# Plain float32 operands in place of products of split float32r parts, in a two-layer diffusion backbone on one core

## The chip, the cores and the metric

One core of a Trainium2 chip runs the whole program, in one launch. The metric is the device time of that launch in microseconds (us), as a median over runs. All inputs and outputs are float32 in the chip's main memory (HBM).

The core's engines are TensorE (PE in the profile, with its weight loads listed apart as PEld), VectorE (DVE), ScalarE (ACT), GpSimd (POOL) and SyncE (SP), which here issues most of the transfers (DMAs). Each engine works through its own list of instructions in order and waits on semaphores for the others.

## What is computed

A backbone of two layers works on 640 tokens of 1024 features: 128 context tokens and 512 latent tokens, which share the weights but have their own modulation (adaLN) and, in the second layer, their own start states.

```
for l in range(2):
    sh1, sc1, g1, sh2, sc2, g2 = split(silu(cond) @ ada_w[l] + ada_b[l], 6)
    h = rmsnorm(x, norm1_g[l]) * (1 + sc1) + sh1
    m = sgu_mixer(h) if l == 0 else rwkv_mixer(h)
    x = x + g1 * m
    h = rmsnorm(x, norm2_g[l]) * (1 + sc2) + sh2
    x = x + g2 * (square(relu(h @ mlp_w1[l])) @ mlp_w2[l])      # 1024 -> 4096 -> 1024
y = rmsnorm(x, final_g)

def sgu_mixer(h):                     # layer 0
    u, v = split(gelu(h @ w_in), 2)   # 1024 -> 2 x 1024
    v = layernorm(v); v = w_s[group] @ v + b_s    # mixes the 128 positions of a chunk
    return (u * v) @ w_out

def rwkv_mixer(h):                    # layer 1: two scans, forward and backward, 16 heads of 64
    xr, xw, xk, xv, xa, xg = [h + shift(h) * mu[j] for j in range(6)]
    r, k, v = xr @ w_r, xk @ w_k, xv @ w_v
    g = sigmoid(xg @ g1) @ g2
    decay, a = low-rank maps of xw and xa, one for each direction   # 1024 -> 64 -> 1024
    y = scan(forward) + scan(backward)   # s = s * w + (s @ -kk) (kk a) + v k;  y = s @ r
    return ((layernorm_of_heads(y) + bonus * v) * g) @ w_o
```

Outputs are the two groups' y and the final scan states of the context.

## The kernel before, in words

Activations lie feature-major: eight tiles of 128 features by 640 tokens. The tokens are taken in two halves, 0 to 256 and 256 to 640 (`HS`). One matmul instruction multiplies a stationary 128x128 weight block with up to 512 moving columns and adds into PSUM.

**The splitting.** float32r is a kind of operand that holds part of a float32 value. Every operand of a large product is cut into a high part (a float32r copy, ScalarE) and a low part (value minus high part, VectorE), and a product of two tiles becomes three matmuls: high by high, high by low, low by high. Weights go through `WPool` (L75): `load` fetches a raw tile of 128x1024, 512 KB, on SP's queue, `split` makes whi and wlo. Activations go through `fill` (L98) or `put` (L1191), which make ahi and alo.

```
85         def split(self, r, n=1024):
88             act.copy(hi[:, :n], r[:, :n])
89             vec.tensor_tensor(out=lo[:, :n], in0=r[:, :n], in1=hi[:, :n], op=ALU.subtract)
...
243            def mm(k, m, hs):
244                (wh, wl), (ah, al) = ws[m], acts[k]
245                for j, (w, x) in enumerate(((wh, ah), (wh, al), (wl, ah))):
246                    mmh(pss[m], w[:, k * P:(k + 1) * P], x, k == 0 and j == 0, k == kt - 1 and j == 2, hs)
```

**Where products of split parts run**, in order of time:

- `sgu` (L287): `zmm` (L302, the matmul is L310) multiplies the 640 tokens with w_in, token-major: five tiles of 128 tokens, stationary, by 512 columns of weights, for 4 blocks of columns and 8 feature tiles. The position mixing (L384) and the transposes after it are plain float32; then `fm` with w_out.
- `fm` (L230) is the general feature-major product, out[n] = W[:, n]^T act: for each output tile n and each of 8 input tiles k, three matmuls on each token half, issued in `mmh` (L112, the matmul is L114). PSUM tiles are called fmps. The weights of the next output tile, or group of tiles, are fetched and split while the present one's products run. `evac` empties PSUM. It serves w_out, both layers' MLPs (`mlp`, L406: 32 output tiles for w1, then w2 in four blocks) and the RWKV layer's k projection.
- `rwkv_project` (L462): the first products of the low-rank maps (L507, PSUM tile l1ps) are plain float32 on 255 and 385 columns. `hidden` (L519) splits their result by putting high and low parts in the two halves of the partitions. `mixed` (L536) makes the shifted inputs and splits them. Then a loop over the eight feature tiles t takes r (`rmm`, L733), v (`vmm`, L744, one step behind, 256 columns) and the second low-rank products (`lora2`, L608: L624 with high weights on all 128 rows, L625 with low weights on 64 rows), whose steps are woven between the others; `finish` (L691) and `prep` (L630) prepare the scans on VectorE, ScalarE and GpSimd. Meanwhile GpSimd works at the first scan group's triangular inverse (`inv_sub`, L838).
- `rwkv_core` (L810): the scans, eight groups (four pairs of feature tiles by two directions), all in plain float32 (L910, L1026 to L1054, and the inverses' L962 and L980). Class `Tail` (L1205) weaves the gates (g2) and the product with w_o into the last two groups by a table of positions, in `early`, `gate`, `late`, `last` and `end`; its products of three go through `mm3` (L1178, the matmul is L1180), its splits through `put` and `Tail.split` (L1221). `ahead` (L1294) fetches and splits the first two w1 tiles of the second MLP, from four halves.

The adaLN products (L122, L323, L1166) are plain float32 with a stationary operand of 32 columns. Buffers come from pools with a fixed count for each kind: 5 raw and 4 split weight pairs in the first part, 3 and 2 in the projections, 4 and 3 in the second MLP. The order of instructions on an engine follows the program with priorities for a few urgent stretches.

Of the kernel before, what the change touches and what calls it, by code (L numbers as in the profile page):

```python
# [7 lines left out]
F32 = mybir.dt.float32  # L8
F32R = mybir.dt.float32r
AF = mybir.ActivationFunctionType  # L10
ALU = mybir.AluOpType
# [4 lines left out]
P = 128  # L16
# [12 lines left out]
def tile_trunk(ctx: ExitStack, tc: tile.TileContext, a: dict):  # L29
# [45 lines left out]
    class WPool:  # L75
        def __init__(self, stack, tag, nraw, nsp, **kw):
            self.raw = Pool(stack, f"wr{tag}", {"r": nraw}, **kw)
            self.sp = Pool(stack, f"ws{tag}", {"h": nsp, "l": nsp}, **kw)

        def load(self, src, n=1024):  # L80
            r = self.raw.tile([P, 1024], F32, tag="r", name="wraw")
            nc.sync.dma_start(out=r[:, :n], in_=src)
            return r

        def split(self, r, n=1024):
            hi = self.sp.tile([P, 1024], F32R, tag="h", name="whi")
            lo = self.sp.tile([P, 1024], F32R, tag="l", name="wlo")
            act.copy(hi[:, :n], r[:, :n])  # L88
            vec.tensor_tensor(out=lo[:, :n], in0=r[:, :n], in1=hi[:, :n], op=ALU.subtract)  # L89
            return hi, lo  # L90

        def get(self, src, n=1024):
            return self.split(self.load(src, n), n)

    def parts(pool, tags=("ah", "al")):
        return pool.tile([P, T], F32R, tag=tags[0], name="ahi"), pool.tile([P, T], F32R, tag=tags[1], name="alo")

    def fill(pt, src, r=(0, T)):  # L98
        hi, lo = (x[:, r[0]:r[1]] for x in pt)
        act.copy(hi, src)  # L100
        vec.tensor_tensor(out=lo, in0=src, in1=hi, op=ALU.subtract)  # L101

    def split_act(pool, src, tags=("ah", "al")):
        pt = parts(pool, tags)
        fill(pt, src)
        return pt
# [10 lines left out]
    def ada_steps(wp, l, u, ui):  # L117
# [8 lines left out]
        tm = wp.sp.tile([P, 16, 32], F32, "h", "adat")  # L126
# [31 lines left out]
    class Norm:  # L158
# [19 lines left out]
        # in two steps, with room for other products while the first one's result is worked on  # L178
# [27 lines left out]
        def apply(self, k, bc, l, w, h, dst=None):  # L206
            r = HS[h]
            if dst is None:
                dst = self.pool.tile([P, 384], F32, tag="nh", name="nh")[:, :r[1] - r[0]]
# [1519 lines left out]
```

## Time and profile before

| what | value |
|---|---|
| runs | 2085.41, 2088.6, 2097.09 us; median 2088.6 |
| profiled execution | span 2109.0 us, from first to last instruction; the page gives no other time for it |
| mean granted TensorE clock | 0.937 |
| TensorE busy | 1991.5 us of 15882 matmul records |
| VectorE, ScalarE, GpSimd busy | 1162.9, 774.5, 389.3 us |
| HBM | 214.67 MB read, 45.22 MB written |

By stage, from the profile's windows (us from the span's start):

| stage | from - to | TensorE busy | VectorE busy | granted clock |
|---|---|---|---|---|
| first norm, gating layer's w_in | 0 - 160 | 143.4 | 73.7 | 1.00 |
| position mixing | 160 - 187 | 25.5 | 17.6 | 1.00 |
| w_out, first MLP | 187 - 705 | 516.6 | 202.0 | 1.00 |
| entry of the RWKV layer | 705 - 764 | 40.9 | 53.0 | 0.80 |
| k projection | 764 - 823 | 58.7 | 45.3 | 0.97 |
| projection loop | 823 - 1072 | 214.8 | 173.5 | 0.84 |
| scans, with the tail's products from 1468 on | 1072 - 1640 | 538.3 | 416.4 | 0.87 |
| second MLP | 1640 - 2086 | 445.0 | 168.5 | 1.00 |
| final norm and output | 2086 - 2109 | 8.4 | 13.0 | 0.71 |

How to read it: times are those of one profiled execution. A matmul's record has a start and a modelled end, and records overlap, so a busy TensorE need not be at its peak; the distance from start to start of neighbouring records says more than their length. The clock is the share of full speed that the throttle granted TensorE. The chain of work is followed back from the last instruction, at each step to what released it; what lies beside the chain costs nothing. "L114" is line 114 of the kernel, and where a helper issues all matmuls, tiles' names tell its callers apart.

### The profile page before, as it was taken

The page shows a single profiled execution, that of the slowest core. Times are in us where ns is not written, and L with a number is a line of the kernel's source. Part 1 is how long each engine was busy: PE and PEld are TensorE (multiplying, and loading weights), DVE is VectorE, ACT ScalarE, POOL GpSimd, SP SyncE. Part 2 cuts the span into 40 slices and gives each one's busy share as a digit, 9 for nine tenths or more (in the row PEclk, how much of TensorE's full clock was granted, in tenths as well). Part 3 has the DMA queues.
Part 4 walks back from the last instruction along what each step waited for, and adds up shares of the span by engine and source line. Part 5 has one row for each costly group of instructions (what it writes and reads, how often), then busy time and mean ns, then how long its engine had stood idle before and what let it go on. Part 6 is the DMA issues. An engine that isn't in the chain of part 4 may idle for free.

```text
span 2109.0 us, 39157 instructions
## 1 busy us (share of the span) xinstructions
PE 1991.5 (94%) x15882; PEld 1739.6 (82%) x15882; DVE 1162.9 (55%) x2308; ACT 774.5 (37%) x1737; POOL 389.3 (18%) x689
## 2 busy tenths in 40 slices
PE   6999999999999789988869999999998999999997
PEld 5777889999999678877747766767787999999996
DVE  5435643333333796766786577787658533333334
ACT  5323531312222255444524444554434522222231
POOL 0000000000000200477551465465201000000000
PEclk9999999999999889987869879998799999999998
DMA  8777352222222033554655444552242222222221
GB/s 286 265 266 233 105 184 80 71 81 70 80 71 75 36 96 121 171 151 129 186 159 175 143 131 148 166 160 80 71 130 76 67 74 75 76 74 77 73 67 51
DMA packets 124438, 254.58 MB, mean 121 GB/s; under 512 B 24417, under 2 KB 63969, under 8 KB 124129
## 3 DMA queue, kind: packets, MB, share of 16 engines
q1 hardware_dynamic: 123824, 251.62, 37.3%
q8 instruction: 125, 2.05, 0.4%
q14 instruction: 57, 0.46, 0.1%
q10 hardware_dynamic: 432, 0.46, 0.1%
HBM read 214.67 MB, written 45.22 MB: 123 GB/s over the span
## 4 chain that ended last, share of the span: by engine, by line
PE 85%; DVE 6%; POOL 3%; ACT 2%; issue 2%; DMA 1%; SPq 0%; DVEq 0%; POOLq 0%; ACTq 0%
PE fmps L114 47%; PE zps L310 6%; PE p L910 4%; PE wops L1180 3%; PE vps L751 2%; PE za L1039 2%; PE za L1026 2%; PE sy L1053 2%; PE sy L1034 1%; PE rps L114 1%; PE trps L932 1%; PE adaps L1166 1%; PE adaps L122 1%; PE sy L1036 1%; PE tps L980 1%
## 5 line engine op out<-in xcount | busy, mean ns | idle before, releaser
L114 PE MATMUL fmps<-ahi,whi 128*128 128x256 f32 (+1 forms) x2272 | 534.6, 310 | 4.9 <-ACT ahi L100 3.1
L114 PE MATMUL fmps<-alo,whi 128*128 128x256 f32 (+1 forms) x2272 | 533.8, 309 | 1.3 <-DVE alo L101 1.3
L114 PE MATMUL fmps<-ahi,wlo 128*128 128x256 f32 (+1 forms) x2272 | 533.8, 309 | 0.0
L114 PEld LDWEIGHTS fmps<-ahi,whi 128*128 128x128 f32 x2272 | 414.4, 188 | 11.0 <-ACT ahi L100 6.3
L114 PEld LDWEIGHTS fmps<-alo,whi 128*128 128x128 f32 x2272 | 415.0, 188 | 2.1 <-DVE alo L101 1.8
L114 PEld LDWEIGHTS fmps<-ahi,wlo 128*128 128x128 f32 x2272 | 415.2, 188 | 1.0 <-issue 0.8
L88 ACT CAST whi<-wraw 128x1024 fp32r<-128x1024 f32 x174 | 182.6, 1050 | 632.6 <-PE fmps L114 538.2
L89 DVE TENSOR_TENSOR wlo<-wraw,whi 128x1024 fp32r<-128x1024 f32 x174 | 214.4, 1233 | 276.2 <-ACT whi L88 276.1
L283 DVE SCALAR_TENSOR_TENSOR x<-fmps,mod,x 128x128 f32<-128x128 f32 (+2 forms) x153 | 74.5, 527 | 305.4 <-PE fmps L114 305.4
L491 POOL TENSOR_TENSOR xx<-h 128x254 f32<-128x254 f32 (+1 forms) x16 | 12.1, 754 | 721.2 <-DVE h L210 706.1
L841 POOL TENSOR_TENSOR inv<-inv 128x220 f32<-128x220 f32 (+29 forms) x217 | 100.7, 464 | 114.4 <-DVE inv L834 57.7
L910 PE MATMUL p<-W,IT 128*128 128x256 f32 x320 | 109.6, 453 | 10.0 <-DVE B L925 5.9
L843 POOL TENSOR_TENSOR inv<-inv 128x220 f32<-128x220 f32 (+29 forms) x217 | 104.5, 482 | 16.9
L1042 ACT ACTIVATE RZ<-za 64x64 f32<-64x64 f32 x320 | 58.4, 214 | 66.7 <-PE za L1039 53.9
L1060 DVE TENSOR_TENSOR RZ<-sy,PC 64x64 f32<-64x64 f32 x256 | 49.4, 219 | 60.2 <-PE sy L1054 52.5
L101 DVE TENSOR_TENSOR alo<-rsq,ahi 128x640 fp32r<-128x640 f32 (+2 forms) x69 | 53.6, 776 | 45.6 <-ACT ahi L100 45.3
L100 ACT CAST ahi<-rsq 128x640 fp32r<-128x640 f32 (+2 forms) x69 | 47.5, 689 | 82.2 <-DVE rsq L435 81.8
L910 PEld LDWEIGHTS p<-W,IT 128*128 128x128 f32 x320 | 57.9, 211 | 22.9 <-DVE B L925 6.3
L1054 PE MATMUL sy<-RZ,B 128*64 128x64 f32 x640 | 72.6, 251 | 0.6 <-ACT RZ L1042 0.6
L1026 PEld LDWEIGHTS za<-RZ,W 128*64 128x64 f32 x640 | 43.5, 154 | 33.8 <-DVE RZ L1060 9.0
L1026 PE MATMUL za<-RZ,W 128*64 128x64 f32 x640 | 62.5, 254 | 8.4 <-DVE RZ L1080 5.9
L1036 PE MATMUL sy<-RZ,W 128*64 128x64 f32 x640 | 69.1, 249 | 0.0
(289 smaller groups left out, 3428.4 us busy)
## 6 DMA issues: line engine op xcount, KB each, us to landing
wraw<-w SPq DMA_DIRECT2D x126, 512.0 KB, 3.5
wraw<-ada SPq DMA_DIRECT2D x64, 512.0 KB, 4.9
W<-dKR SPq DMA_DIRECT2D x80, 256.0 KB, 3.5
adaw<-adac SPq DMA_DIRECT2D x32, 512.0 KB, 4.4
dKR<-zero SPq DMA_DIRECT2D x32, 320.0 KB, 6.3
dKR<-KR SPq DMA_DIRECT2D x32, 320.0 KB, 4.1
dIT<-IT SPq DMA_DIRECT2D x16, 640.0 KB, 3.3
IT<-dIT SPq DMA_DIRECT2D x80, 128.0 KB, 2.9
```

Of the source, the lines that this page charges most:

```text
L88: act.copy(hi[:, :n], r[:, :n])
L89: vec.tensor_tensor(out=lo[:, :n], in0=r[:, :n], in1=hi[:, :n], op=ALU.subtract)
L114: pe.matmul(ps[:, PS0 + t0:PS0 + t1], w, x[:, t0:t1], start=start, stop=stop)
L283: vec.scalar_tensor_tensor(out=X[n][:, t0:t1], in0=ps[:, t0 - r[0]:t1 - r[0]], scalar=mod[l][:, which, n, g:g + 1], in1=X[n][:, t0:t1], op ...
L310: pe.matmul(pss[i], x[:, i * P:(i + 1) * P], w[:, kq * 512:(kq + 1) * 512], start=(k == 0 and j == 0), stop=(k == KT - 1 and j == 2))
L841: eng.tensor_tensor(out=tv, in0=LA[:, s + 1:32, s:s + 1].to_broadcast([P, n, m]), in1=LX[:, s:s + 1, c0:c1].to_broadcast([P, n, m]), op=AL ...
L843: eng.tensor_tensor(out=LX[:, s + 1:32, c0:c1], in0=LX[:, s + 1:32, c0:c1], in1=tv, op=ALU.subtract)
L910: pe.matmul(ps[:, :, 2 * e:2 * e + 2].rearrange("p h s t -> p h (s t)"), IT[:, e], W[:, :, 2 * e:2 * e + 2].rearrange("p h s t -> p h (s t ...
L1026: pe.matmul(za[a0:a0 + 64, 0], W[:, h, 3 * e], RZ[:, ti, h, c], start=True, stop=True)
L1036: pe.matmul(sy[y0:y0 + 64, h], W[:, h, 1 + e], RZ[:, ti, h, c], start=h == 0, stop=False)
L1054: pe.matmul(sy[y0:y0 + 64, h], B[:, h, 3 * e], RZ[:, ti, h, c], start=False, stop=h == 1)
L1180: pe.matmul(ps, u, v, start=start and j == 0, stop=stop and j == 2)
```

## The change

All operands of products are plain float32; nothing is split. Weight tiles are used where they land, and one matmul stands where three stood. `split`, `get`, `parts`, `fill`, `split_act`, `mm3`, `put`, `Tail.split` and their tiles are gone; `acts` makes activation tiles, `Tail.load` loads. What had been written to a tile and then split is written straight to the operand: the norm's `apply`, the MLP's square (the tile rsq is gone), the mixed inputs, the gated y, the hidden values of the low-rank maps. Scores, scans, adaLN products and norms' statistics stay. The core of the diff:

```diff
     class WPool:
-        def __init__(self, stack, tag, nraw, nsp, **kw):
-            self.raw = Pool(stack, f"wr{tag}", {"r": nraw}, **kw)
-            self.sp = Pool(stack, f"ws{tag}", {"h": nsp, "l": nsp}, **kw)
+        def __init__(self, stack, tag, n, **kw):
+            self.raw = Pool(stack, f"w{tag}", {"r": n}, **kw)
...
-        def split(self, r, n=1024):
-            hi = self.sp.tile([P, 1024], F32R, tag="h", name="whi")
-            lo = self.sp.tile([P, 1024], F32R, tag="l", name="wlo")
-            act.copy(hi[:, :n], r[:, :n])
-            vec.tensor_tensor(out=lo[:, :n], in0=r[:, :n], in1=hi[:, :n], op=ALU.subtract)
-            return hi, lo
...
+    def acts(pool, n=1):
+        return [pool.tile([P, T], F32, tag="a", name="a") for _ in range(n)]
...
             def mm(k, m, hs):
-                (wh, wl), (ah, al) = ws[m], acts[k]
-                for j, (w, x) in enumerate(((wh, ah), (wh, al), (wl, ah))):
-                    mmh(pss[m], w[:, k * P:(k + 1) * P], x, k == 0 and j == 0, k == kt - 1 and j == 2, hs)
+                mmh(pss[m], ws[m][:, k * P:(k + 1) * P], xs[k], k == 0, k == kt - 1, hs)
...
                     for i in range(5):
-                        for j, (w, x) in enumerate(((wh, ah), (wh, al), (wl, ah))):
-                            pe.matmul(pss[i], x[:, i * P:(i + 1) * P], w[:, kq * 512:(kq + 1) * 512],
-                                      start=(k == 0 and j == 0), stop=(k == KT - 1 and j == 2))
+                        pe.matmul(pss[i], hs[k][:, i * P:(i + 1) * P], wcur[0][:, kq * 512:(kq + 1) * 512],
+                                  start=k == 0, stop=k == KT - 1)
...
-    MB = (4, 3, 11)
+    MB = (12, 11)
...
                     r = mp.tile([P, T], F32, tag="r", name="relu")[:, :m]
                     act.activation(out=r, in_=ps, func=AF.Relu)
-                    q = mp.tile([P, T], F32, tag="q", name="rsq")[:, :m]
-                    vec.tensor_tensor(out=q, in0=r, in1=r, op=ALU.mult)
                     if n not in ss:
-                        ss[n] = parts(sp)
-                    fill(ss[n], q, rg)
+                        ss[n], = acts(sp)
+                    vec.tensor_tensor(out=ss[n][:, rg[0]:rg[1]], in0=r, in1=r, op=ALU.mult)
...
-            wp = WPool(el, "p", 3, 2)
+            wp = WPool(el, "p", 7)
...
-                            pe.matmul(ps, hi[:, 2 * x + d], hw[:, sl], start=True, stop=False)
-                            pe.matmul(ps, lo[a0:a0 + 64, 2 * x + d], hw[a0:a0 + 64, sl], start=False, stop=True)
+                            pe.matmul(ps, w[a0:a0 + 64, 2 * x + d], hid[x][a0:a0 + 64, sl], start=True, stop=True)
...
-            def rmm(t, raw, z):
-                wh, wl = wp.split(raw)
+            def rmm(t, w, z):
                 ps = pp.tile([P, 1024], F32, "f", "rps")
                 for k in range(KT):
-                    ah, al = xrs[k]
-                    for j, (w, x) in enumerate(((wh, ah), (wh, al), (wl, ah))):
-                        mmh(ps, w[:, k * P:(k + 1) * P], x, k == 0 and j == 0, k == KT - 1 and j == 2)
+                    mmh(ps, w[:, k * P:(k + 1) * P], xrs[k], k == 0, k == KT - 1)
...
-                    self.rings = {"x": (F32, 4, []), "r": (F32, 4, []), "o": (F32, 3, []), "s": (F32R, 6, [])}
+                    self.rings = {"x": (4, []), "r": (4, []), "o": (3, []), "s": (3, [])}
...
+                def load(self, src, n, keep=None):
+                    r = buf(keep, [P, 512], F32, "wos") if keep else self.tmp(n, "s")
+                    nc.sync.dma_start(out=r[:, 0:n], in_=src)
+                    return [r[:, c:c + P] for c in range(0, n, P)]
...
                             for k in range(4):
-                                mm3(ps, ws[n][k], self.ys[k][h], k == 0, k == 3)
+                                pe.matmul(ps, ws[n][k], self.ys[k][h], start=k == 0, stop=k == 3)
...
                 def ahead(self):
-                    w = xw.tile([P, 4, 1024], F32R, "w", "w1s")
-                    nn.pre = [(w[:, 0], w[:, 1]), (w[:, 2], w[:, 3])]
...
+                    w = xw.tile([P, 4, 1024], F32, "w", "w1s")
+                    nn.pre = [w[:, n] for n in range(3)]
+                    for n in range(3):
+                        nc.sync.dma_start(out=nn.pre[n], in_=a["w1"][1, n])
+                        yield
...
-        wp = WPool(es, "a", 5, 4)
+        wp = WPool(es, "a", 12)
```

`vmm` changes like `zmm`, `end` and `finish` of `Tail` like its other products; `WPool(es, "b", MB[0])` of the second MLP holds 12 tiles.

More of the change, by code (lines that the diff above doesn't have):

```diff
@@ L75, in tile_trunk, with tile @@
     class WPool:
-        def __init__(self, stack, tag, nraw, nsp, **kw):
-            self.raw = Pool(stack, f"wr{tag}", {"r": nraw}, **kw)
-            self.sp = Pool(stack, f"ws{tag}", {"h": nsp, "l": nsp}, **kw)
+        def __init__(self, stack, tag, n, **kw):
+            self.raw = Pool(stack, f"w{tag}", {"r": n}, **kw)
+        def tile(self):
+            return self.raw.tile([P, 1024], F32, tag="r", name="w")
         def load(self, src, n=1024):
-            r = self.raw.tile([P, 1024], F32, tag="r", name="wraw")
+            r = self.tile()
             nc.sync.dma_start(out=r[:, :n], in_=src)
             return r
-        def split(self, r, n=1024):
-            hi = self.sp.tile([P, 1024], F32R, tag="h", name="whi")
-            lo = self.sp.tile([P, 1024], F32R, tag="l", name="wlo")
-            act.copy(hi[:, :n], r[:, :n])
-            vec.tensor_tensor(out=lo[:, :n], in0=r[:, :n], in1=hi[:, :n], op=ALU.subtract)
-            return hi, lo
[L92 to L106, printed above, removed]
+    def acts(pool, n=1):
+        return [pool.tile([P, T], F32, tag="a", name="a") for _ in range(n)]
     def segs(r):
@@ L600, in ahead @@
             def ahead(t):
[L601 removed]
+                l2 = ev_.tile([P, 512], F32, "lr", "l2")
                 nc.sync.dma_start(out=l2, in_=a["l2"][t])
@@ L608, in lora2 @@
             def lora2(raw, tiles):
[L609 to L613 removed]
+                w = raw.rearrange("p (a b) -> p a b", a=4)
                 yield
@@ L1174, in ada_core @@
                 gamma(1, 1)
-            def mm3(ps, w, x, start, stop):
-                for j, (u, v) in enumerate(((w[0], x[0]), (w[0], x[1]), (w[1], x[0]))):
-                    pe.matmul(ps, u, v, start=start and j == 0, stop=stop and j == 2)
             def bank(n, tag="p"):
@@ L1212, in tmp @@
                 def tmp(self, n, ring="r"):
-                    dt, size, tiles = self.rings[ring]
+                    size, tiles = self.rings[ring]
                     if len(tiles) < size:
-                        t = buf("B", [P, 512], dt, "tmp")
+                        t = buf("B", [P, 512], F32, "tmp")
                     else:
```

170 lines of the change are left out of this document (55 added, 115 removed).

## The prediction

> **What bounds the kernel now.** The page comes first: who is busy, and what the chain of work that ended last consists of.
>
> ```profile
> span 2109.0 us, 39157 instructions
> PE 1991.5 (94%) x15882; PEld 1739.6 (82%) x15882; DVE 1162.9 (55%) x2308; ACT 774.5 (37%) x1737; POOL 389.3 (18%) x689
> PEclk9999999999999889987869879998799999999998
> ...
> PE 85%; DVE 6%; POOL 3%; ACT 2%; issue 2%; DMA 1%; SPq 0%; DVEq 0%; POOLq 0%; ACTq 0%
> PE fmps L114 47%; PE zps L310 6%; PE p L910 4%; PE wops L1180 3%; PE vps L751 2%; PE za L1039 2%; PE za L1026 2%; PE sy L1053 2%; PE sy L1034 1%; PE rps L114 1%; PE trps L932 1%; PE adaps L1166 1%; PE adaps L122 1%; PE sy L1036 1%; PE tps L980 1%
> ...
> wraw<-w SPq DMA_DIRECT2D x126, 512.0 KB, 3.5
> ```
>
> The reader is to see that TensorE holds 85% of the chain, and that one helper line, L114 (the products of `fm`), holds 47% of the span. Busy time alone proves little for a pipelined engine, so the second view is the list of waits (engine and line, for whom; total, times, longest): do the splits pace the products, or the products the splits?
>
> ```profile
> ACT whi L88 <- PE fmps L114: 538.2, 123, 13.2
> DVE wlo L89 <- ACT whi L88: 276.1, 79, 7.1
> ...
> PE fmps L114 <- ACT ahi L100: 3.1, 1, 3.1
> ...
> PE fmps L114 <- DVE alo L101: 2.1, 3, 1.0
> ```
>
> ScalarE waits 538 us for TensorE to give split buffers back; TensorE waits some 5 us for splits in `fm`. The splits are hidden there, and the products are the pace. So the question is what one product costs in each form.
>
> **Price of the old form.** The chain in order of time (start, length, what) has long unbroken runs of it:
>
> ```profile
> 53.16 17.69 PE zps L310 x75
> ...
> 1649.05 436.45 PE fmps L114 x2974
> ```
>
> 436.45 / 2974 = 0.1468 us a record, mean over 256 and 384 columns (0.459 ns a column). Call a 128x128 weight block with all 640 tokens a pair of `fm`: three products, two token halves, six records, 0.881 us. For `zps` (512 columns) a product is 17.69 / 75 = 0.236 us, a pair of tiles 0.708.
>
> **Price of the new form.** Some products are plain float32 already, the low-rank ones of L507 for one. Rows: groups by shape over the whole span and over 748.5 to 757.5, the stretch's engine times, and two rows of the timeline (start, length from first start to last end, count).
>
> ```profile
> L507 PE MATMUL l1ps<-xq,wraw 128*128 128x385 f32 x48 | 19.3, 566 | 9.9 <-DVE xq L477 9.9
> ...
> 748.50:757.50 9.00, 9.00 (x29) 5.28 (x28) 8.74 (x14) 5.35 (x7) 0.00 (x0) 1.00 0.40 104
> ...
> L507 PE MATMUL l1ps<-xq,wraw 128*128 128x385 f32 x29 | 9.5, 487 | 0.0
> ...
> L507 PEld LDWEIGHTS l1ps<-xq,wraw 128*128 128x128 f32 x28 | 5.3, 190 | 3.7
> ...
> 748.30 3.07 PE L507 MATMUL l1ps<-xq,wraw 128*128 128x385 f32 x9
> ...
> 1122.19 1.13 PE L910 MATMUL p<-W,IT 128*128 128x256 f32 x4
> ```
>
> The code has 3 x 8 = 24 such products of 385 columns and the trace 48 records: a plain product leaves two, each with a weight load. Nine in a row take 3.07 us; without the last one's 0.487 that is 2.58 / 8 = 0.323 us from start to start, 0.839 ns a column. Granted clock 1.00. The four records of L910 bear it out: three gaps of 256 x 0.839 = 0.215 leave 1.13 - 0.64 = 0.49 for the last. The weight loads take no time of their own: 28 of them are busy 5.28 of 9 us beside a TensorE busy 9.00. A 256-column record, 0.215 us, still covers a load of 0.190; without that cover each of a pair's four records would add up to 0.19.
>
> So a pair of `fm` becomes 2 x 640 x 0.839 ns = 1.074 us instead of 0.881: +0.193. Two records at nearly twice the column price replace three: 22% more, not a third less.
>
> **The change part by part.** Counts of products (one form of three is shown, so its count is that of pairs; the 256-column half stands for both):
>
> ```profile
> L114 PE MATMUL fmps<-alo,whi 128*128 128x256 f32 x1136 | 318.1, 280 | 1.3 <-DVE alo L101 1.3
> L114 PE MATMUL fmps<-alo,w1s 128*128 128x256 f32 x16 | 4.5, 283 | 0.0
> ...
> L310 PE MATMUL zps<-whi,alo 128*128 128x512 f32 x160 | 63.9, 399 | 0.0
> L751 PE MATMUL vps<-whi,alo 128*128 128x256 f32 x160 | 50.1, 314 | 0.0
> L625 PE MATMUL zps<-hw,l2l 64*128 64x320 f32 x64 | 28.0, 449 | 3.0 <-DVE l2l L612 3.0
> L114 PE MATMUL rps<-alo,whi 128*128 128x256 f32 x64 | 20.5, 320 | 0.0
> ```
>
> 1. `fm` (w_out, both MLPs, wk): 1136 + 16 = 1152 pairs. At 0.881 they make 1014 us, and the chain gives L114 47% of 2109 = 991: all on the path. 1152 x 0.193 = **+222**.
>
> One page of the Trainium skill speaks against this price. By the Trainium skill, "FP8 and Floating Point Precision", section TensorE Precision Notes, true float32 takes four passes through the array, where the reduced kind reads the 4-byte value and truncates it; with one pass for the reduced kind the ratio is 4 to 3, an estimated 1.174 us a pair, and this term +338. The measured column prices (0.839 x 2 against 0.459) give 3.66 to 3, and the sum goes by them; the other is a rival below.
>
> 2. `zmm` in the gating layer: 160 pairs, 2 x 512 x 0.839 = 0.859 against 0.708: 160 x 0.151 = **+24**. All on the path: 160 x 0.708 = 113 us is 5.4% of the span, and the chain gives L310 6%.
>
> 3. The projection loop (r, v, second low-rank products; 823 to 1072 us). Views: the stretch, the chain's shares in it, and the first and last of the nine splits that lie on its chain.
>
> ```profile
> 823.00:1072.00 249.00, 214.78 (x1279) 178.84 (x1278) 173.47 (x150) 124.61 (x199) 142.83 (x180) 0.84 0.52 154
> ...
> by line: PE vps L751 20.3%; PE rps L114 11.9%; issue 10.8%; PE zps L625 7.0%; POOL AT L841 5.0%; PE zps L624 3.9%; POOL inv L843 3.6%; DVE IT L665 3.5%; DVE IT L663 3.3%; DMA S<-kk 2.8%; PE rbps L114 2.5%; PE bops L726 2.4%; POOL PC L645 2.
> ...
> 836.67 0.94 ACT whi L88
> ...
> 1059.95 1.13 DVE wlo L89
> ...
> 861.11 0.28 PE L751 MATMUL vps<-whi,alo 128*128 128x256 f32 x1
> ...
> 865.91 0.28 PE L751 MATMUL vps<-wlo,ahi 128*128 128x256 f32 x1
> ```
>
> No single engine paces this: chains through VectorE, GpSimd and TensorE alternate, at a granted clock of 0.84. Streaming at full clock: r 64 x 0.193 = 12.4; v, from 0.120 a product (40 starts in 4.80 us), 160 x (0.429 - 0.360) = 11.1; low rank 64 x (2 x 320 x 0.839 ns - 2 x 0.147) = 15.6, since two split records become two plain ones of nearly double length. Together 39, at clock 0.84 46. The chain holds 43.1% of 249 = 107 us of these products, whose streaming is (56.4 + 57.6 + 18.8) / 0.84 = 158: 68% of them. So 0.68 x 46 = 31. From the chain go nine splits, 9.4 us together. Net **+22**; ends -9 (products hidden, splits gone) and +46. VectorE also loses splits off the chain there, which I count at nothing: what is late next is `prep`'s long products (L663, L665).
>
> 4. The tail, 1490 to 1650 (gates and w_o during and after the last scans). By the code 8 + 64 = 72 pairs.
>
> ```profile
> by line: PE wops L1180 44.4%; PE za L1026 6.6%; PE fmps L114 6.0%; PE za L1039 5.4%; PE sy L1053 4.7%; PE sy L1034 4.3%; PE sy L1036 2.6%; PE sy L1054 2.3%; issue 2.1%; PE ytps L1131 1.8%; DVE nh L210 1.7%; DMA tmp<-wo 1.6%; PE tps L980 1.6
> ...
> 1582.44 0.76 DVE alo L1193
> ...
> 1609.31 0.43 DVE yp L1193
> ```
>
> 44.4% of 160 us is 71, at least the 72 x 0.881 = 63 of streaming: on the path. +13.9, less nine splits on the chain from the first to the last row shown, 5.3 us: **+9** (ends -5 and +14). Here loads of w_o reach TensorE without a stop at ScalarE, VectorE or GpSimd, but a load now waits until products release its tile; ring `s` holds three tiles where it held three pairs of parts.
>
> 5. Splits that stand on the chain elsewhere, 14 rows:
>
> ```profile
> 24.09 0.71 ACT ahi L100 x2
> ...
> 1648.66 0.34 DVE alo L101
> ```
>
> 2.4 us before the first `zps`, 3.5 between the mixing products (ScalarE's copy from PSUM stays), 3.5 at the entry of the RWKV layer, 2.7 at the second MLP's first tiles: **-12**. What is late next there is the normalization's own activation.
>
> 6. All other splits, buffers and transfers: 0. The four large groups of splits:
>
> ```profile
> L88 ACT CAST whi<-wraw 128x1024 fp32r<-128x1024 f32 x174 | 182.6, 1050 | 632.6 <-PE fmps L114 538.2
> L89 DVE TENSOR_TENSOR wlo<-wraw,whi 128x1024 fp32r<-128x1024 f32 x174 | 214.4, 1233 | 276.2 <-ACT whi L88 276.1
> L101 DVE TENSOR_TENSOR alo<-rsq,ahi 128x640 fp32r<-128x640 f32 (+2 forms) x69 | 53.6, 776 | 45.6 <-ACT ahi L100 45.3
> L100 ACT CAST ahi<-rsq 128x640 fp32r<-128x640 f32 (+2 forms) x69 | 47.5, 689 | 82.2 <-DVE rsq L435 81.8
> ```
>
> ScalarE loses 230 us and VectorE 268 in them, and `fm`'s part of it lies under its products, as the waits showed: those 5 us are all that could come back. Weights are loaded a tile ahead; a tile now lasts 8 x 1.074 = 8.6 us, and a load lands in 3.5 (the page's last line above). Were that cover gone, each tile would add the difference to TensorE's queue, where every later product stands behind it. On SP's queue nothing is moved past a scan's load but `ahead`'s: three whole w1 tiles in the last scan instead of four half ones, and one load fewer in the MLP behind it. The scans keep their products and are costed at nothing.
>
> Sum: 222 + 24 + 22 + 9 - 12 = +265. On the profiled execution: 2109 + 265 = 2374. The page gives its span alone, 20.4 us above the median of the runs, 2088.6; I carry the difference over: 2088.6 + 265 = **2354 us**, slower by 13%.
>
> **The rivals.**
> Four records' worth at the old price: if plain products in dense streams cost 4/3 of three split ones, term 1 grows by 116, `zps` by 13, the loop by 14, the tail by 7: 2354 + 150 = 2504. For it: 0.839 was seen in stretches of microseconds, not hundreds. Against: the old form shows one column price in both (0.469 in 5 us of `vps`, 0.459 in 436 us of `fm`), and the clock row is 1.00 in the plain stretch. (It is what the section of the Trainium skill named in step 1 would give.)
>
> Loop and tail hide their longer products: the loop gives -9 and the tail -5, 265 - 31 - 14 = 220: 2309. For it: VectorE's 70% and the mixed chain of the loop. Against: 43% of that chain is these very products.
>
> The other side, faster: the L507 rows are paced by their feed, not by TensorE, and a plain record streams at the old column price. For it: VectorE is busy 8.74 of those 9 us, making each moving tile. Then a pair costs four records, 4 x 0.147 = 0.587: 1152 x -0.294 = -338, `zps` -38, splits -27: near 1686. It decides from a record below 0.688 ns a column (0.881 / 1280) on. Against: a product's two records share their operands, so the second needs no feed, yet L910 shows the same spacing inside four records whose tiles were all there. That the products don't change form at all is excluded by the diff.
>
> **How the numbers follow.** Forecast 0.78; hidden loop and tail 0.13; 4/3 price 0.05; faster 0.02; the rest, mostly a tail or loop slower than costed, 0.02. The loop's and tail's ends (-31 / +24, -14 / +5), another 10 us for the column price and the runs' own spread give 2300 to 2405, which leaves out the 4/3 case and the faster one. About 0.5%, 10 us, is what this measurement tells from no change: faster 0.02, within 0.01, slower 0.97.
>
> **What would show it.** Right: L114's `fmps` in one form, 4608 records, 0.215 and 0.322 us apart, two MLP stretches of some 550 us each instead of 451; whi, wlo, ahi, alo gone; ScalarE less busy by 230 us or more and VectorE by 268 or more; the chain still TensorE's. Wrong: records below 0.18 or above 0.23 us apart at 256 columns, TensorE idle between `fm`'s tiles behind a weight DMA, or a granted clock below 0.95 inside the MLPs.

## The result, and the profile after

The changed kernel takes 2308.66 us (median of runs from 2306.0 to 2312.76) against 2092.85 for the kernel before (2085.41 to 2108.12, the runs on the same chip): a ratio of 1.1006 with a 95% interval of 1.0951 to 1.106, slower by 216 us between the medians. The forecast was 2354 in a range of 2300 to 2405. The sign and the size of the large terms came out; the projection loop and the tail came out with the wrong sign.

The page of the changed kernel: span, busy time of the engines, granted clock in 40 slices, shares of the chain, the group of `fm`, and the weight loads (last number: us from issue to landing).

```profile
span 2304.2 us, 32383 instructions
PE 2237.5 (97%) x12982; PEld 1506.4 (65%) x12982; DVE 823.3 (36%) x1942; ACT 492.4 (21%) x1367; POOL 368.7 (16%) x677
PEclk9999999999999988998989998999999999999998
PE 94%; DVE 2%; DMA 1%; ACT 1%; POOL 1%; issue 1%; SPq 0%; DVEq 0%; POOLq 0%; ACTq 0%
...
L95 PE MATMUL fmps<-a,w 128*128 128x384 f32 (+1 forms) x4512 | 1218.2, 433 | 1.5 <-ACT lh L496 1.3
...
w<-w SPq DMA_DIRECT2D x125, 512.0 KB, 3.4
```

VectorE lost 339.6 us of work and ScalarE 282.1; TensorE has 2900 records fewer and is busy 246 us longer. It now holds 94% of the chain (85% before). With 96 further records on the tiles w1s, `fm` has the 4608 that were forecast, and the group shown waits 1.5 us in all. The chain in order of time has the price:

```profile
51.31 21.66 PE zps L283 x50
...
830.60 5.09 DMA w<-g
...
1749.91 529.13 PE fmps L95 x1968
```

529.13 / 1968 = 0.2689 us a record where the old form had 0.1468. A pair of `fm` (four records) takes 1.0755 us; 1.074 was forecast. For `zps`, 21.66 / 50 = 0.433 a record, 0.430 forecast.

By stage, in the two traces, from TensorE's first record of one stage to its first record of the next (us; the last two columns are differences). The entry and the final norm are counted from the last record ahead of them, and the loop ends with its last `vps` record:

```
stage                                     before   after   measured   forecast
start to first zps                          27.9    23.6     -4.3       -2.4
w_in (zps)                                 133.6   157.8    +24.2      +24
position mixing                             23.3    20.6     -2.7       -3.5
w_out, first MLP                           523.5   631.7   +108.2     +111
entry of the RWKV layer                     54.9    57.1     +2.2       -3.5
k projection                                61.6    71.7    +10.1      +12
projection loop                            244.4   229.3    -15.1      +22
last vps to first scan step                 13.1    15.5     +2.4        0
first scan group                            91.8    71.5    -20.3        0
scan groups 2 to 6                         295.4   299.6     +4.2        0
last two groups, and tail behind them      161.7   149.4    -12.3       +9
second MLP                                 460.8   559.2    +98.4      +96
final norm                                  16.7    17.3     +0.6        0
```

The dense stages agree with their forecast within some 3 us each. Most of the deviation stands in three rows: loop, first scan group, tail. Here they are in the windows of the kernel before and then of the changed one. Columns: stretch, its length, busy time (records) of TensorE, weight loads, VectorE, ScalarE, GpSimd, then the granted clock, DMA share and GB/s.

```profile
824.90:1069.40 244.50, 211.87 (x1259) 177.41 (x1260) 170.85 (x146) 122.09 (x195) 141.72 (x178) 0.84 0.52 155
1069.40:1082.50 13.10, 3.16 (x14) 2.05 (x12) 12.35 (x19) 1.21 (x4) 1.17 (x3) 0.72 0.77 213
1082.50:1174.40 91.90, 84.89 (x912) 61.85 (x912) 60.05 (x173) 35.40 (x136) 28.83 (x64) 0.82 0.49 150
...
1469.80:1591.70 121.90, 117.84 (x1352) 95.10 (x1353) 80.22 (x246) 51.37 (x190) 27.61 (x44) 0.87 0.33 100
1591.70:1631.50 39.80, 35.81 (x235) 32.28 (x231) 31.81 (x98) 16.82 (x44) 4.23 (x3) 0.96 0.17 54
```

```profile
962.50:1191.80 229.30, 228.28 (x969) 149.38 (x966) 136.13 (x121) 103.64 (x171) 126.67 (x171) 0.94 0.54 156
1191.80:1207.30 15.50, 8.90 (x35) 5.90 (x33) 14.58 (x19) 2.72 (x6) 12.19 (x15) 0.67 0.78 252
1207.30:1278.70 71.40, 69.95 (x895) 53.12 (x894) 53.68 (x174) 34.06 (x136) 30.24 (x59) 1.00 0.63 186
...
1578.30:1690.00 111.70, 111.40 (x1276) 75.72 (x1274) 66.63 (x227) 35.78 (x161) 19.53 (x44) 0.96 0.37 116
1690.00:1727.70 37.70, 37.70 (x171) 26.88 (x166) 25.85 (x84) 12.07 (x32) 0.00 (x0) 1.00 0.05 15
```

In the loop TensorE was busy 211.87 of 244.5 us at a clock of 0.84, and is now busy 228.28 of 229.3 at 0.94. Busy time times clock is 178 us before and 215 after: the 37 us of additional streaming (39 forecast) are there. They filled the 32.6 us in which TensorE had waited, and the clock rose. The question for the experiments was what shortens the loop, and what the first scan group, whose own products did not change, has to do with it.

### The profile page after: what moved, and what is told of

It is laid out like the page before. It is cut to its first block, busy times and chain, and to the rows that moved or that the text cites. A ratio compares the mean times of both kernels' runs of the same rounds, so it can differ in the third digit from the quotient of the medians.

```text
span 2304.2 us, 32383 instructions
## 1 busy us (share of the span) xinstructions
PE 2237.5 (97%) x12982; PEld 1506.4 (65%) x12982; DVE 823.3 (36%) x1942; ACT 492.4 (21%) x1367; POOL 368.7 (16%) x677
## 4 chain that ended last, share of the span: by engine, by line
PE 94%; DVE 2%; DMA 1%; ACT 1%; POOL 1%; issue 1%; SPq 0%; DVEq 0%; POOLq 0%; ACTq 0%
PE fmps L95 54%; PE zps L283 6%; PE p L856 4%; PE vps L698 3%; PE rps L95 3%; PE zps L578 2%; PE za L972 2%; PE za L985 2%; PE wops L1188 2%; PE sy L999 2%; PE wops L1284 2%; PE sy L980 1%; PE trps L878 1%; PE adaps L1112 1%; PE l1ps L477 1%; PE tps L926 1%
## 5 line engine op out<-in xcount | busy, mean ns | idle before, releaser
L95 PE MATMUL fmps<-a,w 128*128 128x384 f32 (+1 forms) x4512 | 1218.2, 433 | 1.5 <-ACT lh L496 1.3
L95 PEld LDWEIGHTS fmps<-a,w 128*128 128x128 f32 x4512 | 856.2, 190 | 361.2 <-ACT lh L496 1.8
L405 ACT ACTIVATE relu<-fmps 128x640 f32<-128x640 f32 (+2 forms) x70 | 45.8, 657 | 903.2 <-PE fmps L95 903.0
L408 DVE TENSOR_TENSOR a<-relu 128x640 f32<-128x640 f32 (+2 forms) x70 | 53.6, 768 | 490.3 <-ACT relu L405 490.0
L283 PE MATMUL zps<-w,a 128*128 128x512 f32 x320 | 141.9, 598 | 0.0
L787 POOL TENSOR_TENSOR inv<-inv 128x220 f32<-128x220 f32 (+29 forms) x217 | 105.7, 487 | 72.1 <-DVE inv L780 36.5
L283 PEld LDWEIGHTS zps<-w,a 128*128 128x128 f32 x320 | 59.4, 190 | 78.2 <-issue 74.0
L789 POOL TENSOR_TENSOR inv<-inv 128x220 f32<-128x220 f32 (+29 forms) x217 | 105.6, 487 | 16.9
L95 PE MATMUL rps<-a,w 128*128 128x256 f32 (+1 forms) x256 | 82.9, 478 | 0.0
L698 PE MATMUL vps<-w,h 128*128 128x256 f32 x320 | 77.4, 389 | 0.0
L698 PEld LDWEIGHTS vps<-w,h 128*128 128x128 f32 x320 | 58.3, 190 | 20.1 <-issue 12.9
L95 PEld LDWEIGHTS rps<-a,w 128*128 128x128 f32 x256 | 51.7, 209 | 30.1 <-issue 12.6
L972 PEld LDWEIGHTS za<-RZ,W 128*64 128x64 f32 x640 | 42.3, 144 | 32.6 <-issue 9.1
```

The lines of the kernel that those rows point to most:

```text
L95: pe.matmul(ps[:, PS0 + t0:PS0 + t1], w, x[:, t0:t1], start=start, stop=stop)
L283: pe.matmul(pss[i], hs[k][:, i * P:(i + 1) * P], wcur[0][:, kq * 512:(kq + 1) * 512], start=k == 0, stop=k == KT - 1)
L408: vec.tensor_tensor(out=ss[n][:, rg[0]:rg[1]], in0=r, in1=r, op=ALU.mult)
L698: pe.matmul(pss[i // 2][:, i % 2], xvs[k][:, i * P:(i + 1) * P], w[:, kq * 256:(kq + 1) * 256], start=(k == 0 and i % 2 == 0), stop=(k == ...
L787: eng.tensor_tensor(out=tv, in0=LA[:, s + 1:32, s:s + 1].to_broadcast([P, n, m]), in1=LX[:, s:s + 1, c0:c1].to_broadcast([P, n, m]), op=AL ...
L789: eng.tensor_tensor(out=LX[:, s + 1:32, c0:c1], in0=LX[:, s + 1:32, c0:c1], in1=tv, op=ALU.subtract)
```

## The experiments

### One part at a time

Four kernels exchange the projection loop, or loop and tail, between the two forms. `mid_split` and `loop_split` have the dense stages plain, as in the changed kernel, `mid_plain` and `loop_plain` have them split, as in the one before. The exchange, shown for the r projection (v, the low-rank products and, in the tail, `mm3` alike):

```diff
-            def rmm(t, raw, z):
-                wh, wl = wp.split(raw)
+            def rmm(t, w, z):
...
-                    ah, al = xrs[k]
-                    for j, (w, x) in enumerate(((wh, ah), (wh, al), (wl, ah))):
-                        mmh(ps, w[:, k * P:(k + 1) * P], x, k == 0 and j == 0, k == KT - 1 and j == 2)
+                    mmh(ps, w[:, k * P:(k + 1) * P], xrs[k], k == 0, k == KT - 1)
```

`mid_split`, the dense stages plain, loop and tail split:

> The changed kernel with the projection loop and the tail put back to products of split parts; the dense products stay plain. Stages of the two known traces: the changed kernel is 15 us shorter in the loop, 16 in the scans and 14 in the tail than before, where the forecast had +22, 0 and +9. Theory A (these 45 us come from the loop's and the tail's own change): the loop is about 244 us again, the tail 122, and the time 2309 + 45 = 2354. Theory B (they come from what lies around: clock left over from the longer dense streams, earlier weights, a lighter VectorE elsewhere): loop near 229 and time within 10 of 2309.

`loop_split`, all plain but the loop:

> The changed kernel with only the projection loop (r, v, second low-rank products) put back to split parts. Theory A: loop 244 us instead of 229, and the first scan group 92 instead of 71, if that group's gain is a late effect of the loop: 2309 + 15 + 16 = 2340; if the scans' gain is not the loop's, 2309 + 15 = 2324. Theory B: within 8 of 2309.

`mid_plain`, the dense stages split, loop and tail plain:

> The kernel before with the loop's and the tail's products plain; the dense products (gating layer, w_out, MLPs, k projection) stay split. Theory A: 2093 - 45 = 2048, loop about 229, tail about 112, granted clock in the loop 0.94 instead of 0.84. Theory B: within 10 of 2093; and by the forecast's own terms (+22, +9) 2124.

`loop_plain`, all split but the loop:

> The kernel before with only the loop's products plain. Theory A: 2093 - 15 - 16 = 2062 if the first scan group's gain follows the loop, 2078 if not. By the forecast's term 2115. Theory B: within 8 of 2093.

Measured, beside 2090.86 for the kernel before on that chip:

```
kernel       loop    tail    median us   ratio to before (95%)     loop   first scan group   last two groups
mid_split    split   split   2329.3      1.1122 (1.1062-1.1181)    239.6       91.7              111.9
loop_split   split   plain   2323.69     1.1094 (1.1038-1.115)     239.5       91.8              111.3
mid_plain    plain   plain   2070.05     0.9887 (0.983-0.9945)     231.0       71.6              111.6
loop_plain   plain   split   2081.56     0.9939 (0.9912-0.9965)    231.0       71.6              113.1
```

Making only the dense stages plain costs 2329.3 - 2090.86 = 238 us, where the terms of `fm`, `zmm` and the splits elsewhere make 234. A plain loop gains 9 us with the dense stages split (2090.86 - 2081.56) and 15 with them plain (2323.69 - 2308.66); loop and tail together gain 21 in both cases. The 2308.66 is from the round above, where the kernel before took 2 us longer, so differences with it are uncertain by about that much. Neither "they cost 31" nor "they cost nothing" is what happens. Theory A had the stages right and the times too far apart (45 and 31 us, where 21 and 9 to 15 came): its differences were those of the two traces, and that of the kernel before is longer than any of its timed runs. `loop_split` came out at the 2324 that was expected if the scans' gain were not the loop's, yet its first scan group took 91.8 us, so that agreement is luck. The first scan group follows the form of the loop ahead of it: 92 us behind a split loop, 71 to 72 behind a plain one. And `mid_plain` is faster than both kernels.

### What sets the loop

`dead_splits` puts back the work of the splits for ScalarE and VectorE without the use of their results: in the changed kernel's loop, w_r, w_v and the second low-rank weights are cut into two parts that no product reads. `few_tiles` takes the buffers back to three weight tiles and one low-rank tile. `lr_twice` issues each of the 64 second low-rank products twice into the same PSUM tile.

```diff
+            def cast(r, n):
+                hi = dead.tile([P, 1024], F32R, "h", "dhi")[:, 0:n]
+                lo = dead.tile([P, 1024], F32R, "l", "dlo")[:, 0:n]
+                act.copy(hi, r[:, 0:n])
+                vec.tensor_tensor(out=lo, in0=r[:, 0:n], in1=hi, op=ALU.subtract)
```

```diff
-            wp = WPool(el, "p", 7)
+            wp = WPool(el, "p", 3)
...
-            ev_ = Pool(el, "rpv2", {"vs": 2, "lr": 2})
+            ev_ = Pool(el, "rpv2", {"vs": 2, "lr": 1})
```

```diff
-                            pe.matmul(ps, w[a0:a0 + 64, 2 * x + d], hid[x][a0:a0 + 64, sl], start=True, stop=True)
+                            for _ in range(2):
+                                pe.matmul(ps, w[a0:a0 + 64, 2 * x + d], hid[x][a0:a0 + 64, sl], start=True, stop=True)
```

> The changed kernel, with the loop's splits of weights (w_r, w_v, second low-rank weights) made again by ScalarE and VectorE into tiles that no one reads: 2.7 us of ScalarE and 3.6 of VectorE more in each of the eight steps, with no product behind them. Theory R (relief: the loop became shorter, 244 to 229 us, since the splits left ScalarE's and VectorE's queues): the loop goes back towards 240, TensorE idle again for 20 us or more, time about 2320. Theory C (cover: TensorE's own longer products now set the loop's length, at 228 of 229 us busy, and the other engines' work lies under them): loop within 4 us of 229, time within 6 of 2309.

> The changed kernel with three weight tiles instead of seven in the projections and one low-rank tile instead of two. Theory B (buffers: weights lie ready earlier, and that took TensorE's waits away): loop 240 or more, TensorE waiting for DMAs of wr and wv, time 2320 or more. Theories R and C: loop within 4 us of 229, time within 6 of 2309.

> The changed kernel with each of the 64 second low-rank products issued twice into the same PSUM tile: 64 x 0.537 = 34 us of streaming more in the loop, nothing else. Theory C: the loop is TensorE's, 229 + 34 = 263 at the same mean clock of 0.94, 250 if the clock comes to 1.00; time 2330 to 2343. If the loop is still paced by chains through VectorE and GpSimd: loop below 240, time below 2320.

The loop's window of the three, in that order:

```profile
961.40:1195.50 234.10, 229.65 (x968) 151.55 (x966) 160.39 (x138) 118.55 (x190) 143.77 (x171) 0.93 0.51 150
```

```profile
959.70:1196.60 236.90, 235.95 (x969) 151.42 (x966) 138.64 (x121) 104.07 (x171) 125.50 (x171) 0.92 0.55 161
```

```profile
962.20:1226.30 264.10, 261.32 (x1097) 171.69 (x1094) 142.68 (x121) 104.53 (x171) 126.06 (x171) 0.95 0.47 136
```

Twice the low-rank products lengthen the loop by 34.8 us, about their whole streaming, and the kernel by 30 (2338.36, ratio 1.1151, 1.1099 to 1.1202): the plain loop is TensorE's. Fewer buffers leave the time where it was (2307.15, 1.0996, 1.0946 to 1.1046); the loop of the profiled execution is 7.6 us longer, at a clock of 0.92, with TensorE idle for 1 us as in the changed kernel. That is outside the 4 us of theories R and C and short of the 240 of theory B, and no wait for weights came with it. Unread splits with 24 us of VectorE's time lengthen the loop by 5, yet the kernel by 15 (2323.84, 1.108, 1.103 to 1.1129). No theory had a place for the other 10. The stage marks put it right behind the loop: from the last `vps` to the first scan step it took 33.9 us, against 15.5 in the changed kernel.

`mid_lr_split` asked from the other side whether a still shorter TensorE helps: `mid_plain` with the low-rank products split again.

```diff
-                            pe.matmul(ps, w[a0:a0 + 64, 2 * x + d], hid[x][a0:a0 + 64, sl], start=True, stop=True)
+                            pe.matmul(ps, hi[:, 2 * x + d], hw[:, sl], start=True, stop=False)
+                            pe.matmul(ps, lo[a0:a0 + 64, 2 * x + d], hw[a0:a0 + 64, sl], start=False, stop=True)
```

> The kernel before with loop and tail plain (2070 us), but the second low-rank products split again, two records of 0.147 us in place of two of 0.269: 15.6 us of streaming less, 8 us of VectorE and 5 of ScalarE more. Theory C: loop 231 - 16 = 215, time 2054. Theory R: the split's waits come back, loop 231 to 244, time 2070 or more.

It failed as a forecast: 2086.64 (0.9951, 0.9932 to 0.997) instead of 2054. Theory R's "2070 or more" fits the time, but not for its reason, since the loop became shorter. Its loop, and the stretch from the last `vps` to the first scan step:

```profile
826.50:1052.20 225.70, 218.23 (x968) 153.69 (x966) 138.88 (x126) 106.91 (x177) 129.93 (x171) 0.95 0.54 157
1052.20:1086.10 33.90, 11.84 (x40) 8.15 (x38) 30.80 (x53) 3.24 (x7) 28.45 (x45) 0.62 0.49 144
```

The loop fell by 5 us only, with 7.5 us of idle TensorE again: TensorE paces it by a small margin. And again 33.9 us pass behind it, with VectorE busy for 30.8 of them.

### The order on VectorE behind the loop

Put together, the stretch from the last `vps` to the second scan group takes 102.6 to 107.2 us in every kernel that makes any split in the loop (before, `mid_split`, `loop_split`, `dead_splits`, `mid_lr_split`, and `tail_plain` below) and 86.9 to 87.1 in every one that makes none (after, `mid_plain`, `loop_plain`, `few_tiles`, `lr_twice`). What VectorE does there, in groups over the 36 us behind the last `vps` of the kernel before (count, busy us, mean ns, idle of the engine before them and its releaser):

```profile
L910 PE MATMUL p<-W,IT 128*128 128x256 f32 x29 | 13.5, 609 | 10.0 <-DVE B L925 5.9 <-DMA IT<-dIT 4.1
...
L843 DVE TENSOR_TENSOR inv<-inv 128x98 f32<-128x98 f32 (+9 forms) x14 | 7.3, 525 | 0.4
L841 DVE TENSOR_TENSOR inv<-inv 128x98 f32<-128x98 f32 (+9 forms) x14 | 6.9, 495 | 0.3
L923 DVE TENSOR_TENSOR W<-p,cst 64x128 f32<-64x128 f32 x12 | 3.5, 289 | 0.8 <-PE p L910 0.6
```

L841 and L843 are the pieces of the second group's triangular inverse; L923 and L925 empty the scores p from PSUM for the first group's steps. TensorE waits 5.9 us for B (L925). In the traces of the split kernels VectorE has 18 or 19 of the inverse's instructions between one eviction and the next, or ahead of the first. In the plain kernels piece and eviction alternate. The end of the row in the kernel before, and VectorE at the same place in the changed one (L869 and L871 are its evictions, L787 and L789 its pieces):

```profile
1092.31 0.65 DVE L841 TENSOR_TENSOR inv<-inv 128x108 f32<-128x108 f32 x1
1092.99 0.64 DVE L843 TENSOR_TENSOR inv<-inv 128x108 f32<-128x108 f32 x1
1093.66 0.59 DVE L923 TENSOR_TENSOR W<-p,cst 64x128 f32<-64x128 f32 x2
```

```profile
1211.60 0.41 DVE L871 TENSOR_TENSOR B<-p,cst 128x256 f32<-128x256 f32 x1
1211.93 0.28 DVE L789 TENSOR_TENSOR inv<-inv 128x38 f32<-128x38 f32 x1
1212.24 0.59 DVE L869 TENSOR_TENSOR W<-p,cst 64x128 f32<-64x128 f32 x2
```

The source has the same order in all of them: the build arranges the instructions, and it arranges them otherwise when the loop ahead is another.

Three kernels undo that order and leave every product as it was. Four one-column copies tie the pieces to the evictions:

```diff
-            spread(lx[1][1], *DVI)
+            pcs = lx[1][1]
+
+            def after_ev(i, f):
+                def g():
+                    vec.tensor_copy(inv[:, 4648:4649], fr[0].buf[fr[0].units[i]][1][:, 0, 0, 0:1])
+                    f()
+                return g
+
+            for s, i in ((0, 3), (2, 5), (4, 6), (6, 7)):
+                pcs[s] = after_ev(i, pcs[s])
+            spread(pcs, *DVI)
```

> The kernel before with every product split, but with one thing moved: in the first scan group, VectorE's pieces of the second group's inverse no longer stand in one row ahead of the evictions of the scores p. Four one-column copies from B tie the pieces to the evictions, so that eviction and piece alternate as in the changed kernel. Order theory: from the last vps to the second scan group it takes 105 us in every kernel that splits anything in the loop and 87 in every one that does not; the cause is that row on VectorE, and the granted clock of 0.50 there follows from the idle TensorE. Then the stretch falls to about 87 us here too, the loop stays at 244, and the time is 2091 - 18 = 2073. Clock theory: the split loop itself leaves the clock low, the order does not matter; the stretch stays near 105 and the time at 2091.

> The kernel before with loop and tail plain but the low-rank products split, and with the same reordering of VectorE's inverse pieces. Order theory: the loop stays at 226 us, the stretch from the last vps to the second group goes from 107 to about 87, and the time from 2087 to about 2068, at or a little below the 2070 of the kernel with loop and tail plain. Clock theory: 2087.

> The changed kernel with splits in the loop that no product reads, as in the earlier run, and the same reordering of VectorE's inverse pieces. Order theory: the loop stays at 234 us, the stretch from the last vps to the second group falls from 105 to about 87, and the time from 2324 to about 2309 plus the loop's 5, or 2306 to 2313. If the splits' own time on VectorE and ScalarE were what costs: it stays at 2324.

The stretch fell in all three: from 104.9 to 87.6, from 107.2 to 89.7, and from 104.8 to 89.8. The windows of `before_order` (loop, hand-over, first scan group, last two groups):

```profile
827.70:1065.20 237.50, 207.24 (x1258) 174.51 (x1259) 171.55 (x146) 122.24 (x195) 141.90 (x178) 0.86 0.53 159
1065.20:1078.40 13.20, 2.88 (x15) 1.96 (x13) 12.35 (x19) 1.31 (x4) 1.17 (x3) 0.74 0.77 211
1078.40:1152.80 74.40, 73.16 (x910) 55.31 (x910) 54.14 (x177) 34.82 (x136) 31.59 (x64) 0.98 0.61 185
...
1450.00:1572.80 122.80, 118.60 (x1352) 95.76 (x1352) 79.25 (x247) 51.57 (x190) 29.88 (x49) 0.86 0.33 98
```

With all splits in place, the first scan group is 17.5 us shorter and its clock is 0.98 instead of 0.82. So it was the order on VectorE that made this stretch long, and the low clock went with it. In hand-over and first group together, TensorE's busy time falls from 88.1 to 76.0 and its idle time from 17.0 to 11.6: two thirds of the gain are records that stream at a higher clock.

The kernel times follow the stretch only roughly:

```
kernel          median us   ratio to before (95%)      order theory   without the order
before_order    2088.29     0.9963 (0.9941-0.9986)       2073            2091
mid_lr_order    2056.5      0.9822 (0.9793-0.985)        2068            2087
dead_order      2300.19     1.0976 (1.0944-1.1007)       2306-2313       2324
```

`dead_order` gained 24 us and `mid_lr_order` 30 where the stretch gave 15 to 18. Their traces are 33 and 28 us apart, and the rest lies there in scan groups 2 to 6, which took 300.1 and then 282.5 us, and 294.3 and then 284.8. Here they are for `dead_splits` and `dead_order`:

```profile
1300.30:1600.40 300.10, 296.19 (x3765) 206.15 (x3765) 227.40 (x709) 141.10 (x566) 160.81 (x339) 0.91 0.46 141
```

```profile
1286.00:1568.50 282.50, 279.68 (x3773) 197.01 (x3773) 229.52 (x709) 142.14 (x568) 168.57 (x349) 0.95 0.48 150
```

VectorE's instructions stand in another order in these groups too, and the granted clock is higher. The four copies thus changed more than the one row, and this part of the gain is not the row's. `before_order` gained 7 us by the medians (2095.1 to 2088.29) and not the 18 expected, with runs from 2077 to 2096. In its profiled execution the last two groups stand at a clock of 0.86 and take 122.8 us (the row above), as in the profile of before; with the same split tail `mid_split` had this row, and `loop_plain` took 113.1 at 0.96:

```profile
1593.20:1705.10 111.90, 108.25 (x1353) 87.56 (x1352) 79.21 (x248) 48.60 (x187) 23.01 (x41) 0.98 0.39 116
```

So a split tail can lose some 10 us to the clock. The runs of `before_order` spread with it as well: 2076.89 us at a mean clock of 0.956, 2096.34 at 0.942. Whether the new order makes a slow tail likelier is open.

### The tail alone

`tail_plain` is the kernel before with only the tail's products plain:

```diff
-                            for k in range(4):
-                                mm3(ps, ws[n][k], self.ys[k][h], k == 0, k == 3)
+                            for k in range(4):
+                                pe.matmul(ps, ws[n][k], self.ys[k][h], start=k == 0, stop=k == 3)
```

> The kernel before with only the tail (gates and w_o in the last two scan groups and behind them) plain. By the prediction's step 4: 9 us slower than before, 2100. By the rival that the tail hides its longer products: 5 us faster at most, 2086. By the medians of the earlier pairs with and without a plain tail: 6 to 11 us faster, 2080 to 2085. The loop and the first scan group stay at 244 and 92 us in each case.

2086.53 us against 2095.1, ratio 0.9956 (0.9937 to 0.9975): faster by 9 us, between 5 and 13. The loop took 236.6 us and the first scan group 89.3, less than the 244 and 92 expected, though nothing in them was changed. Last two groups, and the tail behind them:

```profile
1456.50:1569.90 113.40, 112.65 (x1268) 76.36 (x1266) 66.89 (x230) 37.68 (x164) 17.96 (x37) 0.97 0.37 112
1569.90:1607.20 37.30, 37.30 (x167) 26.45 (x163) 25.27 (x81) 12.19 (x32) 0.00 (x0) 1.00 0.07 22
```

Behind the last group `end` issues 32 pairs: 28.2 us of streaming at 0.881 in a stretch of 39.8 when split, 34.4 at 1.0755 in 37.3 when plain. The split form left 11.6 us there that its streaming did not fill; 6.2 us more streaming fit in, and the splits ahead of each product are gone. These are 2.5 us. The other 8.5 us by which the trace is shorter lie in the last two groups, where a split tail took anything from 111.9 to 122.8 us with the clock; why the medians differ by 9 us is shown for the 2.5 only.

## Why the prediction came out as it did

**Price, right.** The views that gave it were the spacing of plain records in a stretch of 9 us and the long runs of the chain; 1.0755 us a pair was measured for 1.074, and it held over 529 us of unbroken products at a clock of 1.00. The rival of 4/3, 1.174 us a pair, is excluded by that row. The sentence of the Trainium skill it came from ("FP8 and Floating Point Precision", TensorE Precision Notes: four passes for true float32) says nothing of the reduced kind's pace; here three reduced products to one plain one stand as 0.881 to 1.0755.

**Steps 1, 2 and 5, right but for one term.** Dense stages alone cost 238 us by `mid_split` against 234. In step 5 the entry of the RWKV layer was to give 3.5 us back and took 2.2 more: its splits left the chain, and the wait for the weights (w<-g, 5.09 us at 830.60 on the chain) came in their place. It was not priced.

**Step 3, wrong in sign: +22 forecast, 15 us faster in the traces.** Over all traces the loop with every product split takes 236.5 to 244.4 us; the plain one takes 229.3 to 231.0, and 236.9 with fewer buffers. The medians of the kernels with only the loop exchanged, 9 and 15 us, hold the stretch behind the loop too and do not give the loop alone. The additional streaming was right (39 forecast, 37 found). The step took the chain's 68% as the part that must lengthen the loop and kept the old idle time and the old clock of 0.84 for the rest. Neither stayed. Of 249 us TensorE was idle for 34 and the chain alternated between engines; longer products filled those gaps, and a TensorE without gaps was granted 0.94. `lr_twice` shows that the new loop is TensorE's. `dead_splits` gives two thirds of the splits' time on VectorE back without a product that waits for it, and the loop grows by 5 only: this points to the products' waits for their parts, more than to VectorE's load, as what the old loop lost. No run took those waits away alone. The end of -9 was on record for exactly this ("products hidden, splits gone").

**"The scans keep their products and are costed at nothing", wrong by 18 us in the traces.** The stretch from the last `vps` to the second scan group fell from 104.9 to 86.9. `before_order` reproduces it without any change of a product: the build's order on VectorE is the cause. Of its 17 us the kernel's median showed 7. No rival had it. Costing unchanged instructions at nothing left out that their order is worked out anew in each build.

**Step 4, wrong in sign: +9 forecast, 9 us faster in `tail_plain`.** The products' share of the tail's chain, 44%, was read as a TensorE at its pace; the 39.8 us behind the last group held 28.2 of streaming. That accounts for 2.5 us; the rest of the gain goes with the clock of the last two groups and is not explained. The step's end of -5, hidden products and no splits, was the nearer one.

**The carried-over difference.** The 20.4 us by which the profiled span of before lies above the median of its runs were carried over, as if the changed kernel would keep them. It did not: its span of 2304.2 lies 4.5 below its median. The profiled execution of before, 2109.0 us, is longer than every timed run of that kernel. It had a tail at a low clock (121.9 us at 0.87, where `mid_split` took 111.9) and the longest split loop of five (244.4; the others 236.5 to 239.6). So the traces differ by 195 us and the medians by 216.

Sum over the medians: 238 for the dense stages, some -12 for the loop with what follows it, -9 for the tail: 217, measured 216. How the -12 divide between the loop and the order behind it, the medians do not tell. The rival "loop and tail hide their longer products" had 2309, almost the measured value, and its mechanism for the loop was the right one; but it priced loop and tail together at -14 where they gave -21 with the stretch between them, against which the dense terms' 4 us stand, and it knew nothing of the order on VectorE. That its sum comes out within 1 us is luck. The forecast itself stayed inside its range because the range had the hidden loop and tail as its lower end; its middle was 45 us too high.

**What was to show it.** 4608 records, splits gone, ScalarE 282 us less busy (230 or more), VectorE 340 (268 or more), the second MLP at 559.2, the chain TensorE's: all as written. None of the signs of a wrong forecast appeared in the dense stages.

**The better version.** `mid_plain`, split where TensorE streams without a break and plain in loop and tail, takes 2070.05 (0.9887, 0.983 to 0.9945). With the low-rank products split and the order on VectorE tied, `mid_lr_order` takes 2056.5 (0.9822, 0.9793 to 0.985), the fastest here.

## What to carry to other kernels

Price an operand's form by records from start to start, and then ask of each stage whether TensorE streams there without a gap: three split products beat one plain float32 product by 18% of its time in the dense stages and lost to it in the loop, where other engines set the pace. In a mixed stage, take the busy time off the length of the stretch first; that remainder and the granted clock can absorb longer products, and a share of the chain cannot tell that. Where a build arranges instructions itself, compare the order on each engine in the stages behind the change, too: one row of 18 small instructions lengthened the stretch behind the loop by 17 us here, though only 7 of them came off the kernel's median when the row was broken up.

## What the runs showed of the hardware

A granted clock of 0.50 can outlast the wait that brought it on. In the kernel before, in the first scan group (three of the 5 us windows; TensorE 0.36 of 5 busy, then busy throughout):

```profile
1090.00:1095.00 5.00, 0.36 (x1) 0.36 (x2) 4.78 (x10) 0.00 (x0) 4.37 (x9) 0.73 0.89 307
1095.00:1100.00 5.00, 5.00 (x80) 3.46 (x81) 4.26 (x12) 0.83 (x2) 4.45 (x8) 0.50 0.02 5
...
1110.00:1115.00 5.00, 5.00 (x33) 3.58 (x32) 2.07 (x8) 3.41 (x10) 3.90 (x15) 0.50 0.40 106
```

and in `before_order`, where the wait is gone:

```profile
1085.00:1090.00 5.00, 5.00 (x97) 3.96 (x94) 3.38 (x12) 1.90 (x5) 4.45 (x8) 1.00 0.93 303
```

The clock stayed at 0.50 for 20 us, from 1095 to 1115, although the records leave TensorE no gap. The Trainium skill, "TensorE: Matmul & The Clock Gate", section What's actually happening, has the half clock and lets the full one return after about 3.4 us of sustained work. The half clock agrees with the row; the 20 us do not agree, unless these small products, whose ends the profile models, do not count as sustained work, and no run here separates the two. The granted clock also moves stages whose products are the same: the last two scan groups with a split tail took 121.9 and 122.8 us at 0.87 and 0.86 (before, `before_order`), and 111.9 and 113.1 at 0.98 and 0.96 (`mid_split`, `loop_plain`).
